# A Griffin-style encoder step on one core: splits in two steps, loads and in-place sums set apart, buffers given homes that outlast a stage

## The chip, the cores and the metric

The kernel runs on one core of a Trainium2 chip. The metric is the device time of one execution in microseconds (us). The engines that matter are TensorE (PE for its matmuls, PEld for its weight loads), VectorE (DVE), ScalarE (ACT), GpSimd (POOL) and SyncE (SP). Each works through its own list of instructions in order and waits for the others by semaphores. SP issues nearly all loads, POOL issues most of the stores to scratch memory in the later stages.

## The reference

One layer of a streaming encoder is applied to 2048 frames of a new stream and to 64 frames of a running one; the kernel treats the 2112 frames as one row of columns, with channels in the partitions.

```python
proj = rmsnorm(x, norm_mix) @ w_in                       # 1024 -> 5632
x_rnn, y_gate, q, k, v, g_rnn, g_attn = jnp.split(proj, cuts, axis=-1)
h = rg_lru(causal_dwconv(x_rnn, ...), ...)               # a linear recurrence over time
y_attn = band_attention(rope(q), rope(k), v, sinks)      # chunks of 64, window 128
mixed = sigmoid(g_rnn) * h * gelu(y_gate) + sigmoid(g_attn) * y_attn
x = x + mixed @ w_out                                    # 1024 -> 1024
up = causal_dwconv(rmsnorm(x, norm_ffn) @ w_up, ...)     # 1024 -> 5632, three taps
gate, val = jnp.split(up, 2, axis=-1)
y = rmsnorm(x + (silu(gate) * val) @ w_down, norm_final) # 2816 -> 1024
```

All of it is float32, and the results (y, the key and value caches, the states) are float32.

## The kernel before

**Products.** A float32 operand is taken apart into a high part (ACT copies it, rounded, into an fp32r tile: `split`, L198) and a low part (DVE subtracts the high part from the source: L199). Each product is three matmuls, high by high, high by low, low by high. The function `split` issues both instructions one after the other, so the low part on DVE waits for ACT at once.

**Four stages.** (A) The product with `w_in`, the attention and the recurrence run over three sets of columns (`SETS`); here a scheduler orders the instructions by dependencies. From there on the order is the order in which the code is written ("manual schedule"). (B) The product with `w_out` runs in three phases, one for each pair of column blocks (`PAIRS`: 304, 304 and 448 columns a block). In a phase, `wout(i, m)` makes one of 8 output rows in two halves j; the weights come as 256 KB of `w_out`, are split (`wsplit`, L381) and kept in scratch `woS`, from which the later phases load them (`wload`, L371). Beside it run generators, driven a few steps at a time by `drive`: `mixes(p)` (L347) loads the rows of the mixed result for the next pair and splits them, `xprep(p)` (L769) loads the new residual rows, norms them, makes Strassen-like sums and splits those. `residual` (L848) adds the residual input, stores `x1S` and collects the squares for the norm. (C) The product with `w_up` goes by a plan of units; a unit has seven steps u, one of the seven block products of a Winograd scheme each (`Lane.product`, matmuls at L1040 to L1042). The first 20 units make their weights afresh and have two lanes (pairs 0 and 1, 24 matmuls a step); four units with one lane follow (12 matmuls a step), then 11 units of pair 2 with two lanes. `prepare` makes the weights a few steps ahead (raw loads L885, sums L907, splits; or a load of kept ones from `wuS`, L903). `Lane.after(u)` (L1079) takes the partial sums p1, p7 and V out of PSUM (ACT, L1087), adds (DVE, L1091 to L1098), starts the convolution (ACT L1070, DVE L1076), then SiLU (L1109), the gate (L1114) and the sums of the hidden rows (L1123 to L1132), which POOL stores to `hS` (L1119). `at(d, f)` puts a piece d steps later. (D) The product with `w_down` runs over seven products i and the pairs p, eleven k each (matmuls L1470 to L1472); `dweight` makes weights, `parts` splits hidden rows, and `side` drives the residual adds (`resid`), the squares (L1435 to L1439), the last norm (L737 to L739) and the outputs (L1452, L1454).

**Waits inside the lists.** Where an ACT split waits for its load, all that stands behind it on ACT waits too; the same holds for a DVE low part that waits for ACT. In stage B `mixes` has 8 row buffers for pair 0 and 2 for the others, raw weights have 2 buffers. In stage C the first 20 units have one buffer for V, so the second lane's V is taken one step later than the first's:

```python
if u in (0, 1) or u == 2 + (one and self.second_lane):
    i = min(u, 2)
    t = up["s"].tile([P, n], F32, name=("p1", "p7", "V")[i], bufs=1 if i == 2 and one else 2)
```

**Memory.** `Region` is a piece of SBUF that stays open while `Pool`s take slots from it by name. Region FW (23,712 bytes a partition) is opened only when stage A's pools are closed.

Of the kernel before, what the change touches and what calls it, by code (L numbers as in the profile page):

```python
# [126 lines left out]
def kernel(ctx: ExitStack, tc: tile.TileContext, xT, w_in, w_out, w_up, w_dn, gw, pk,  # L127
# [22 lines left out]
    es0 = ExitStack()  # L150
    wpool = es0.enter_context(tc.tile_pool(name="wpool", bufs=2))
# [48 lines left out]

    turn = [0]

    def kept(m, si):
# [6 lines left out]
        raw = wpool.tile([P, KO * P], F32, name="wraw", bufs=2)  # L210
# [25 lines left out]
    def stats(t0, n):  # L236
        r = rp_.tile([P, BN], F32, name="nr", bufs=2)[:, :n]
        s = rp_.tile([P, BN], F32, name="ns", bufs=2)[:, :n]
        for k in range(KO):
            x = xp.tile([P, BN], F32, name="xk", bufs=4)[:, :n]  # L240
# [15 lines left out]
    def apply(t0, n):  # L256
        hi, lo = xslots(t0)
        r = rstd[t0]
        for k in range(KO):
            x = xp.tile([P, BN], F32, name="xk", bufs=4)[:, :n]  # L260
# [86 lines left out]
    def mixes(i, xk):  # L347

        for t0, n in PAIRS[i]:
            xblocks[t0] = mixp[i].tile([P, KO, 2, n], F32R, name=f"x{t0}")  # L350
# [11 lines left out]
        yield  # L362
        for j, (k, t0, n) in enumerate(todo):
            split(xblocks[t0][:, k, 0], xblocks[t0][:, k, 1], raw[j])
            load()
            yield

# [11 lines left out]

    def wsplit(j):  # L380
# [7 lines left out]
    for si, blocks in enumerate(SETS):  # L388
# [282 lines left out]
        for g in range(4):  # L671
# [18 lines left out]
            if g == 3 and si == 2:  # L690

                es0.close()
                FW = Region(tc, "FW", 23712, F32)
                RA = Region(tc, "RA", 58368, F32R)
                mixp, wh0, raws, xk = [Pool(RA), None, None], Pool(RA), Pool(FW), Pool(FW)
                sums = [Pool(FW, right=i == 0) for i in range(3)]
                for i in (2, 1, 0):
                    sums[i].reserve("rs", PAIRS[i][0][1], 2)
                wh0.reserve("wh", 8 * P, 4)
                raws.reserve("wraw", 4 * P, 2)  # L700
                xk.reserve("xk", BS, 8)
# [3 lines left out]
                wload(1)  # L705
            for _ in at:
                if g == 3 and si == 2:
                    next(mixed)
# [58 lines left out]
    def put(p, o, k, src):  # L767
        split(xops[p, o][:, k, 0], xops[p, o][:, k, 1], src)

    def xprep(p, names, rs, tp):  # L770
# [16 lines left out]
        yield  # L787
        for k in range(4):
# [3 lines left out]
            for o in ("11", "21", "22"):  # L792
                if o in names:
                    put(p, o, k, x[o])
            yield
            nc.vector.tensor_tensor(x["11"], x["12"], x["11"], op=ALU.subtract)
            if xt is not None:
                nc.vector.tensor_tensor(x["12"], x["22"], x["12"], op=ALU.subtract)
                nc.vector.tensor_tensor(xt, x["22"], x["11"], op=ALU.subtract)
                load(k + 1, "22")  # L800
                nc.vector.tensor_tensor(x["21"], x["21"], xt, op=ALU.subtract)
                yield
                put(p, "T2", k, xt)
                put(p, "T4", k, x["21"])
                load(k + 1, "21")
                yield
            else:
                load(k + 1, "22", "21")
            if "T1" in names:
                put(p, "T1", k, x["11"])  # L810
            load(k + 1, "11")
            if xt is not None:
                put(p, "T3", k, x["12"])
            load(k + 1, "12")
# [5 lines left out]
    io, tp = [Pool(FW) for _ in phases], Pool(FW)  # L820

    wnext, xres = [3], {}
# [9 lines left out]
    def wout(i, m):  # L832
        work = [(t0, n, xres.pop((t0, m)), acc()) for t0, n in phases[i]]
        for j in (16 * i + 2 * m, 16 * i + 2 * m + 1):
            w = weights.pop(j)
# [8 lines left out]
            while wnext[0] < 48 and wnext[0] <= j + (4 if wnext[0] > 15 else 3):  # L844
                wload(wnext[0])
                wnext[0] += 1
        return work

    def residual(i, m, work):
        for t0, n, xr, ps in work:  # L850
            nc.vector.scalar_tensor_tensor(xr, ps[:, :n], 0.5, xr, op0=ALU.mult, op1=ALU.add)
            nc.gpsimd.dma_start(x1S[m, :, t0:t0 + n], xr)
            if m == 0:
# [33 lines left out]

    def wops(g, fresh):

        r = {"11": wraw(g, "11")}  # L890

        def parts(src):
            t = wh.tile([P, 2, 4 * P], F32R, name="wh")
            split(t[:, 0], t[:, 1], src)
            return t

        def kept_s(i, src):
            if fresh:
                t = parts(src())
                nc.gpsimd.dma_start(wuS[g, i], t.bitcast(F32))  # L900
            else:
                t = wh.tile([P, 2, 4 * P], F32R, name="wh")
# [7 lines left out]
        if fresh:  # L910
            r["21"] = wraw(g, "21")
        yield None
        r["22"] = wraw(g, "22")
        yield parts(r["11"])
        yield kept_s(0, lambda: comb("11", "11", "21", ALU.subtract))
        r["12"] = wraw(g, "12")
# [6 lines left out]
    def wsums(g, pool, out):  # L923

        for h in range(2):
# [5 lines left out]

            def keep(i, src):
                t = out.tile([P, 2, 2 * P], F32R, name="wx", bufs=2)
                split(t[:, 0], t[:, 1], src)
                nc.gpsimd.dma_start(wuS[g, i][:, :, h * 2 * P:(h + 1) * 2 * P], t.bitcast(F32))
# [6 lines left out]
            yield  # L942
            nc.vector.tensor_tensor(a, c, a, op=ALU.subtract)
            keep(1, a)
            yield
            nc.vector.tensor_tensor(b, b, c, op=ALU.add)
            keep(2, b)
            yield
            nc.vector.tensor_tensor(d, d, a, op=ALU.subtract)
            keep(3, d)  # L950
            yield

    def xsums(p, pool, width):
# [700 lines left out]
```

## Time and profile before

| what | value |
|---|---|
| median of 3 runs | 3159.97 us (3152.78 to 3161.12) |
| the profiled execution | 3154.25 us, span 3152.5 us |
| PE busy / DVE busy / ACT busy | 2909.8 / 2073.0 / 1547.2 us |
| matmuls | 17640 |
| mean granted TensorE clock | 0.965 |

The span is the time from the first to the last instruction; the execution's own time is 1.75 us more. A busy PE is not PE at its peak: a matmul at a lower granted clock is busy for longer. In a row of busy times by stretch, the columns are the stretch, its length, the busy time and the count of instructions of PE, PEld, DVE, ACT and POOL, the granted clock, the busy share of the 16 DMA engines and the GB/s that they moved. In a row of waits stand who waited, for whom, the total, how often, and the longest.

### The profile page before, as it was taken

How to read it: one execution, taken by the hardware profiler on the slowest of the kernel's cores; microseconds unless marked ns; L12 is line 12 of the kernel's file. 1: busy time of each engine (PE TensorE's matmuls, PEld its weight loads, DVE VectorE, ACT ScalarE, POOL GpSimd, SP SyncE). 2: the span in 40 equal slices, each digit the busy share in tenths (PEclk: the TensorE clock that was granted, in tenths of full speed). 3: DMA queues.
4: the chain of work that ended last, by engine and by line, in shares of the span. 5: the costliest groups of instructions: out<-in, count | busy, mean ns of one | idle time of the engine just before them, and what ended most of it. 6: DMA issues, size and time to landing. Idle time of an engine off the chain costs nothing. (4 is left out here: it accounts for less than half of the span.)

```text
span 3152.5 us, 48907 instructions
## 1 busy us (share of the span) xinstructions
PE 2909.8 (92%) x17640; PEld 2788.1 (88%) x17640; DVE 2073.0 (66%) x4048; ACT 1547.2 (49%) x3426; POOL 449.8 (14%) x655
## 2 busy tenths in 40 slices
PE   8999999999999999977887999889899998999996
PEld 7988889999989999976787899889799997899995
DVE  5388781577781777753567888777666556567666
ACT  4577662666751776642224444445444444333432
POOL 3231211000000000012211333222101111000001
PEclk9999999999999999987898999999999999999998
DMA  7776547444336444356654556555876666876653
GB/s 245 262 233 194 178 148 251 150 132 133 125 116 216 144 139 142 117 178 234 216 190 166 194 196 212 179 188 179 276 253 213 220 215 181 258 217 207 182 167 110
DMA packets 324499, 595.37 MB, mean 189 GB/s; under 512 B 37168, under 2 KB 224544, under 8 KB 307360
## 3 DMA queue, kind: packets, MB, share of 16 engines
q1 hardware_dynamic: 285728, 461.45, 46.1%
q0 software_dynamic: 38528, 130.79, 11.2%
q8 instruction: 139, 2.28, 0.3%
q14 instruction: 104, 0.85, 0.1%
HBM read 400.99 MB, written 191.64 MB: 188 GB/s over the span
## 5 line engine op out<-in xcount | busy, mean ns | idle before, releaser
L223 PE MATMUL mm<-xh,whl 128*128 128x320 f32 (+2 forms) x2112 | 689.7, 327 | 11.0 <-ACT xh L198 5.4
L224 PE MATMUL mm<-xl,whl 128*128 128x320 f32 (+2 forms) x2112 | 688.8, 326 | 7.4 <-DVE xl L199 4.7
L225 PE MATMUL mm<-xh,whl 128*128 128x320 f32 (+2 forms) x2112 | 686.5, 325 | 1.4 <-POOL whl L199 1.4
L198 ACT ACTIVATE RE<-FW 128x512 fp32r<-128x512 f32 (+2 forms) x540 | 290.1, 558 | 491.0 <-DVE FW L907 97.0
L199 DVE TENSOR_TENSOR RE<-FW,RE 128x512 fp32r<-128x512 f32 (+2 forms) x540 | 315.7, 602 | 210.8 <-ACT RE L198 209.0
L223 PEld LDWEIGHTS mm<-xh,whl 128*128 128x128 f32 x2112 | 401.3, 190 | 18.7 <-ACT xh L198 8.4
L224 PEld LDWEIGHTS mm<-xl,whl 128*128 128x128 f32 x2112 | 401.2, 190 | 16.6 <-DVE xl L199 7.1
L225 PEld LDWEIGHTS mm<-xh,whl 128*128 128x128 f32 x2112 | 401.8, 190 | 2.3 <-POOL whl L199 1.6
L1040 PE MATMUL mf<-RA,RE 128*128 128x304 f32 (+1 forms) x608 | 202.7, 333 | 37.9 <-ACT FA L1087 33.9
L1470 PE MATMUL mf<-RE 128*128 128x304 f32 (+2 forms) x616 | 198.2, 322 | 9.2 <-ACT RE L198 9.2
L1042 PE MATMUL mf<-RA,RE 128*128 128x304 f32 (+1 forms) x608 | 200.2, 329 | 0.3 <-DVE RE L199 0.2
L1041 PE MATMUL mf<-RA,RE 128*128 128x304 f32 (+1 forms) x608 | 199.5, 328 | 0.0
L1471 PE MATMUL mf<-RE 128*128 128x304 f32 (+2 forms) x616 | 198.4, 322 | 0.1
L1472 PE MATMUL mf<-RE 128*128 128x304 f32 (+2 forms) x616 | 196.9, 320 | 0.0
L1040 PE MATMUL mf<-RE 128*128 128x304 f32 (+1 forms) x488 | 161.1, 330 | 15.5 <-ACT FA L1087 11.7
L1042 PE MATMUL mf<-RE 128*128 128x304 f32 (+1 forms) x488 | 160.1, 328 | 0.1
L1041 PE MATMUL mf<-RE 128*128 128x304 f32 (+1 forms) x488 | 159.7, 327 | 0.0
L1040 PEld LDWEIGHTS mf<-RA,RE 128*128 128x128 f32 x608 | 116.2, 191 | 48.1 <-ACT FA L1087 40.2
L1076 DVE SCALAR_TENSOR_TENSOR FW<-FA,pkt,FW 128x608 f32<-128x608 f32 x176 | 146.2, 850 | 18.3 <-ACT FW L1070 15.2
L199 POOL TENSOR_TENSOR gl<-gr,gh 128x256 fp32r<-128x256 f32 x24 | 22.3, 930 | 788.7 <-ACT gh L198 788.7
L1040 PE MATMUL mm<-RE 128*128 128x304 f32 (+1 forms) x392 | 128.1, 327 | 3.3 <-DMA RE<-wuS 3.1
L1042 PE MATMUL mm<-RE 128*128 128x304 f32 (+1 forms) x392 | 126.9, 324 | 2.6 <-DVE RE L199 2.6
(339 smaller groups left out, 7313.0 us busy)
## 6 DMA issues: line engine op xcount, KB each, us to landing
whl<-wiS SPq DMA_DIRECT2D x88, 1024.0 KB, 5.2
RE<-wuS SPq DMA_DIRECT2D x104, 512.0 KB, 4.4
wiS<-whl SPq DMA_DIRECT2D x44, 1024.0 KB, 4.8
wuS<-RE POOLq DMA_DIRECT2D x80, 512.0 KB, 3.2
FW<-in_w_up_dram SPq DMA_DIRECT2D x158, 256.0 KB, 4.8
hS<-FA POOLq DMA_DIRECT2D x154, 152.0 KB, 3.9
FW<-hS SPq DMA_DIRECT2D x154, 152.0 KB, 2.9
wraw<-in_w_in_dram SPq DMA_DIRECT2D x44, 512.0 KB, 5.8
```

The lines of the kernel that those rows point to most:

```text
L198: nc.scalar.activation(hi, src, AF.Copy)
L199: (lo_eng or nc.vector).tensor_tensor(lo, src, hi.bitcast(F32), op=ALU.subtract)
L223: nc.tensor.matmul(ps[:, :n], wh[:, c], xh[:, k, :n], start=first, stop=False)
L224: nc.tensor.matmul(ps[:, :n], wh[:, c], xl[:, k, :n], start=False, stop=False)
L225: nc.tensor.matmul(ps[:, :n], wl[:, c], xh[:, k, :n], start=False, stop=last)
L1040: nc.tensor.matmul(ps[:, :n], w[:, 0, c], x[:, k, 0], start=first, stop=False, **more)
L1041: nc.tensor.matmul(ps[:, :n], w[:, 0, c], x[:, k, 1], start=False, stop=False, **more)
L1042: nc.tensor.matmul(ps[:, :n], w[:, 1, c], x[:, k, 0], start=False, stop=last, **more)
L1076: nc.vector.scalar_tensor_tensor(uc, G[:, j:j + self.cols], col("fw", 44 * j + m), uc, op0=ALU.mult, op1=ALU.add)
L1470: nc.tensor.matmul(ps[m][:, cs], w[:, 0, c], t[:, 0], start=k == 0, stop=False)
L1471: nc.tensor.matmul(ps[m][:, cs], w[:, 0, c], t[:, 1], start=False, stop=False)
L1472: nc.tensor.matmul(ps[m][:, cs], w[:, 1, c], t[:, 0], start=False, stop=k == 10)
```

## The change

The matmuls and what they compute stay; what moves is the place of the instructions in the lists, and the buffers.

- **Splits in two steps.** `split2` issues the high part on ACT and hands back a function that issues the low part on DVE. The callers keep it (`wlow`, `plow`, `dlow`, `low`) and issue it one step later: weights of `w_out` and `w_up`, hidden rows and weights of `w_down`, the rows of `mixes`, `xprep`, `xread`, `wsums`.
- **Stage B.** The generators are driven inside `wout`, after each half j (`besides`), two steps at a time, no longer after the residual (5 or 4 steps). `mixes(1)` has 5 row buffers, `mixes(2)` has 3 and moves from phase 0 to phase 1. Raw weights have 3 buffers and are loaded four halves ahead. The residual of row m-1 stands ahead of the product of row m.
- **First mixed rows early.** FW is opened at the start and also serves stage A. The 16 row loads of pair 0 and two `w_out` loads are written at the second head group of the third set, and the scheduler puts them around the change from the second to the third set, one weight load at the kernel's start. Their splits still go to region RA, which is opened where it was, in the room of stage A's weights and operands.
- **Stage C.** V has two buffers, and both lanes take it at u = 2. The pieces of the convolution are put one step later, ACT's part into `later` (ahead of the products), DVE's part into `then` (behind the preparing of weights). Raw weights are asked for one step earlier, in-place sums stand 3 to 6 steps behind the stores of the same tile. `xprep` of pair 1 is spread over the first four steps, five pieces of one k each. Of the 28 rows that `xread` brings for pair 2, 16 are split beside the one-lane units and 12 beside pair 2's first unit, as before; 19 loads stand in the one-lane units, before 16.
- **Stage D.** The first product goes over the pairs in the order 2, 0, 1; its raw weights are loaded from five steps before the end of stage C, and its weights and first hidden rows are made by the end. `side` takes two steps a k from the fifth product on. The order that emptied `side` at 33 steps before the end (L1497) is gone.

```diff
+    def split2(hi, lo, src):
+        nc.scalar.activation(hi, src, AF.Copy)
+        return lambda: nc.vector.tensor_tensor(lo, src, hi.bitcast(F32), op=ALU.subtract)
...
     def wsplit(j):
         if j < 16:
             weights[j] = t = wh0.tile([P, 2, 4 * P], F32R, name="wh")
-            split(t[:, 0], t[:, 1], wraws.pop(j))
-            nc.gpsimd.dma_start(wpart(j), t.bitcast(F32))
+            low = split2(t[:, 0], t[:, 1], wraws.pop(j))
+            wlow.append(lambda: (low(), nc.gpsimd.dma_start(wpart(j), t.bitcast(F32))))
...
-    def wout(i, m):
+    def wout(i, m, beside):
         work = [(t0, n, xres.pop((t0, m)), acc()) for t0, n in phases[i]]
         for j in (16 * i + 2 * m, 16 * i + 2 * m + 1):
+            while wlow:
+                wlow.pop(0)()
...
-            while wnext[0] < 48 and wnext[0] <= j + (4 if wnext[0] > 15 else 3):
+            while wnext[0] < 48 and wnext[0] <= j + 4:
                 wload(wnext[0])
                 wnext[0] += 1
+            beside()
...
-            residual(i, m, work)
-            drive(side, 5 if i == 0 else 1 if m == 0 else 4)
+            work = wout(i, m, besides if i == 0 or m > 0 else lambda: drive(side, pace[0] if i == 1 else 0))
...
-            if u in (0, 1) or u == 2 + (one and self.second_lane):
-                i = min(u, 2)
-                t = up["s"].tile([P, n], F32, name=("p1", "p7", "V")[i], bufs=1 if i == 2 and one else 2)
+            if u in (0, 1, 2):
+                name = ("p1", "p7", "V")[u]
+                t = up["s"].tile([P, n], F32, name=name)
...
-                self.uv = self.conv_a(self.Gv, vm)
-                at(1, lambda: self.conv_b(self.Gv, vm, self.uv))
+                at(1, lambda: setattr(self, "uv", self.conv_a(self.Gv, vm)))
+                at2(1, lambda: self.conv_b(self.Gv, vm, self.uv))
...
     def prepare(i):
+        while plow:
+            plow.pop(0)()
...
+           for p in ((2, 0, 1) if i == 0 else (0, 1, 2) if i < 6 else (2, 1)) for k in range(11)]
...
         if j == len(seq) - 33:
-            drive(side, 99)
             nc.scalar.activation(warm, epst, AF.Sqrt)
```

**How the lists move.** ACT in phase 0 of stage B, before. RA with 128x512 is a half of the weights, RE and RC with 128x304 or 128x448 are mixed rows of pairs 1 and 2, L858 squares a residual row.

```order
L198 ACTIVATE RE<-FW 128x304 x5
L198 ACTIVATE RA<-FW 128x512 x2
L858 ACTIVATE FW<-FW 128x304 x2
L198 ACTIVATE RE<-FW 128x304 x2
L198 ACTIVATE RE<-FW 128x448
L198 ACTIVATE RC<-FW 128x448
L198 ACTIVATE RA<-FW 128x512 x2
```

ACT at the same place now; `split2` is L205, the squares are L880 and L883.

```order
L205 ACTIVATE RE<-FW 128x304
L205 ACTIVATE RA<-FW 128x512
L205 ACTIVATE RE<-FW 128x304 x2
L880 ACTIVATE FW<-FW 128x304 x2
L205 ACTIVATE RA<-FW 128x512
L205 ACTIVATE RE<-FW 128x304 x2
L205 ACTIVATE RA<-FW 128x512
```

Ahead of two halves of the weights stood five or four mixed rows; now two rows stand between one half and the next, and the 448-wide rows are gone from this phase.

ACT in one of the 20 fresh units, steps u = 0 to 4, before. L198 is the high part of the weights being prepared, L1087 takes p1, p7 or V out of PSUM, L1109 is SiLU.

```order
L198 ACTIVATE RE<-FW 128x512
L1087 ACTIVATE FA<-mf 128x304 x2
L1109 ACTIVATE FA<-FW 128x608 x2
L198 ACTIVATE RE<-FW 128x512
L1087 ACTIVATE FA<-mf 128x304 x2
L198 ACTIVATE RE<-FW 128x512
L1087 ACTIVATE FA<-mf 128x304
L198 ACTIVATE RE<-FW 128x512
L1087 ACTIVATE FA<-mf 128x304
L198 ACTIVATE RE<-FW 128x512
```

The same steps now; L205 is the high part, L1137 the copy out of PSUM, L1153 SiLU.

```order
L205 ACTIVATE RE<-FW 128x512
L1137 ACTIVATE FW<-mf 128x304 x2
L1153 ACTIVATE FA<-FA 128x608 x2
L205 ACTIVATE RE<-FW 128x512
L1137 ACTIVATE FW<-mf 128x304 x2
L205 ACTIVATE RE<-FW 128x512
L1137 ACTIVATE FW<-mf 128x304 x2
L205 ACTIVATE RE<-FW 128x512 x2
```

The second lane's V stood behind the next weights, one step after the first lane's; now the two stand together.

DVE near the end of stage D, before. L1439 adds squares, L1505 adds the last product of pair 1, L739 is the reciprocal of the norm, L1452 writes outputs.

```order
L1439 TENSOR_TENSOR FD<-FD 128x304 x3
L1505 TENSOR_TENSOR RR<-mf,RR 128x304 x4
L199 TENSOR_TENSOR RE<-FW,RE 128x304
L1439 TENSOR_TENSOR FD<-FD 128x304 x3
L1439 TENSOR_TENSOR FD<-FD 128x448 x7
L739 RECIPROCAL FD<-FD 128x448
L1452 SCALAR_TENSOR_TENSOR RR<-RR,pkt,FD 128x448 x8
L1439 TENSOR_TENSOR FD<-FD 128x304 x4
L739 RECIPROCAL FD<-FD 128x304
```

The same place now; L206 is the low part of hidden rows, L1558 adds squares, L1631 is the product's add, L754 the reciprocal, L1571 the outputs.

```order
L1558 TENSOR_TENSOR FD<-FD 128x448
L206 TENSOR_TENSOR RE<-FW,RE 128x304
L1558 TENSOR_TENSOR FD<-FD 128x448 x6
L1631 TENSOR_TENSOR RR<-mf,RR 128x304 x4
L206 TENSOR_TENSOR RE<-FW,RE 128x304 x3
L754 RECIPROCAL FD<-FD 128x448
L1571 SCALAR_TENSOR_TENSOR RR<-RR,pkt,FD 128x448
L206 TENSOR_TENSOR RE<-FW,RE 128x304
L1571 SCALAR_TENSOR_TENSOR RR<-RR,pkt,FD 128x448 x2
```

Before, the squares and the whole output of one block stood in one piece behind the last product of pair 1; now the squares stand ahead of that product's adds, and the low parts of hidden rows, which the next matmuls need, stand between the outputs.

More of the change, by code (lines that the diff above doesn't have):

```diff
@@ L1351 @@
             f()
+        if lanes[0] == (0, 2) and u == 3:
+            for pool in up["c"], up["u"], up["h"]:
+                pool.close()
+            up["c"], up["u"], up["h"] = Pool(FA), Pool(FA), Pool(FP)
+            up["c"].reserve("G", 2 * BM + 2, 3)
+            up["u"].reserve("uc", 2 * BM + 2, 4)
         for lane in live:
             lane.product(u, ready[i, lane.g])
-        while made <= i + ahead:
+        while made < len(plan) + 1 and fits(i):
             prepare(made)
             made += 1
+        for f in then.pop(i, ()):
+            f()
         for lane in live:
@@ L1405, in flushing @@
     def flushing():
[L1406 to L1410 removed]
+        for f in due():
+            f()
+            yield
     dp = R = None
```

484 lines of the change are left out of this document (285 added, 199 removed).

## The prediction

> **What bounds the kernel now.** I read the page's head first, then the span in slices, then the busy times cut at the stages' borders, then the waits inside each stretch.
>
> ```profile
> span 3152.5 us, 48907 instructions
> PE 2909.8 (92%) x17640; PEld 2788.1 (88%) x17640; DVE 2073.0 (66%) x4048; ACT 1547.2 (49%) x3426; POOL 449.8 (14%) x655
> PE   8999999999999999977887999889899998999996
> PEclk9999999999999999987898999999999999999998
> ```
>
> PE bounds the kernel, with 92% of the span. What an order can win lies where the PE slices fall below 9: slices 18 to 22 and 26 to 29 (stages B and C), 34 (the start of stage D), and the last. In most of the same slices the granted clock falls too. The stretches, cut at the stage borders, show by how much; the last two lie in the middle of undisturbed work and give the pace.
>
> ```profile
> 1369.80:1479.30 109.50, 74.99 (x384) 70.56 (x385) 41.98 (x84) 33.38 (x71) 28.82 (x48) 0.74 0.68 223
> 1479.30:1554.40 75.10, 60.92 (x391) 60.00 (x390) 44.30 (x95) 21.69 (x49) 17.47 (x32) 0.89 0.70 229
> 1554.40:1635.90 81.50, 79.06 (x390) 72.78 (x389) 42.56 (x81) 17.13 (x35) 17.53 (x32) 1.00 0.65 213
> 1635.90:1693.20 57.30, 34.20 (x198) 32.39 (x198) 38.66 (x65) 18.81 (x44) 5.40 (x10) 0.76 0.45 150
> 1693.20:2197.90 504.70, 463.05 (x3170) 453.65 (x3169) 394.41 (x680) 238.52 (x564) 150.20 (x276) 0.97 0.55 191
> 2197.90:2263.60 65.70, 53.68 (x338) 51.08 (x337) 43.56 (x73) 32.71 (x75) 10.18 (x19) 0.92 0.82 267
> 2263.60:2642.00 378.40, 375.41 (x1850) 346.74 (x1848) 232.65 (x340) 173.57 (x427) 39.81 (x74) 1.00 0.67 222
> 2642.00:2710.00 68.00, 51.23 (x313) 48.88 (x313) 38.96 (x69) 26.77 (x60) 7.37 (x14) 0.90 0.76 224
> 2710.00:3060.00 350.00, 349.36 (x2141) 335.86 (x2140) 227.87 (x444) 133.06 (x273) 11.51 (x22) 1.00 0.70 208
> 3060.00:3152.50 92.50, 61.91 (x403) 57.49 (x401) 53.57 (x103) 21.88 (x53) 13.44 (x25) 0.84 0.31 97
> 1700.10:1713.60 13.50, 13.47 (x96) 13.47 (x97) 10.82 (x20) 5.02 (x13) 4.81 (x9) 1.00 0.53 189
> 2320.00:2400.00 80.00, 80.00 (x396) 74.16 (x395) 50.12 (x74) 33.49 (x84) 9.16 (x17) 1.00 0.68 223
> ```
>
> At clock 1.00 a 304-wide matmul takes 13.50/96 = 0.1406 us, a 448-wide one 80/396 = 0.202. Length less count times pace is what a stretch loses. Phase 0 of `w_out`: 109.5 - 384 x 0.1406 = 55.5. Phase 1: 75.1 - 391 x 0.1406 = 20.1. Phase 2: 81.5 - 390 x 0.202 = 2.7. The start of `w_up`: 57.3 - 27.8 = 29.5. The other fresh units: 504.7 - 445.7 = 59.0; at 168 matmuls a unit these are 18.87 units of 26.75 us, over a floor of 23.6. The one-lane units: 65.7 - 47.5 = 18.2. Pair 2 of `w_up` and the middle of stage D lose almost nothing (PE busy 375 of 378, 349 of 350). At the start of stage D, PE stands idle for 16.8.
>
> Part of each loss is clock, not idle time. Busy PE over the floor is 21.0 in phase 0, 5.9 in phase 1, 6.4 at the start of `w_up`, 17.4 in the fresh units, 6.2 in the one-lane units, together 57 us. The clock is low just where PE waited, so a wait that goes takes its share of this along. The Trainium skill, "TensorE: Matmul & The Clock Gate", section "What's actually happening", says that for modelling the ramp costs under 1% of a typical kernel's span, which here would be an estimate of 31.5 us; the trace does not agree, with 57 us in five stretches, since the ramp comes again after each long wait. By the page the sum below would be some 25 us less gain, 3057.
>
> **Phase 0 of `w_out`.** The waits in this stretch, the DMA issues by kind, and two ACT rows of the timeline:
>
> ```profile
> PE mf L840 <- ACT RA L198: 29.6, 6, 7.5
> PE mm L840 <- ACT RA L198: 9.2, 2, 4.9
> ACT RA L198 <- DMA FW<-in_w_out_dram: 30.6, 7, 6.0
> ACT RE L198 <- DMA FW<-mixS: 24.0, 9, 4.1
> FW<-mixS SPq DMA_DIRECT2D x16, 224.0 KB, 2.6
> 1385.86 0.97 ACT L198 ACTIVATE RE<-FW 128x304 fp32r<-128x304 f32 x2 [4.07 <-DMA FW<-mixS]
> 1389.86 0.61 ACT L198 ACTIVATE RA<-FW 128x512 fp32r<-128x512 f32 x1
> ```
>
> PE waits 38.8 us for the high parts of weights, and ACT, which makes them, stands 24.0 us at mixed rows whose loads have not landed and 30.6 at raw weights. The timeline shows one case: a mixed row waits 4.07 us, and the weights behind it come at 1389.86. The change puts two rows ahead of a half where four or five stood, more row buffers behind them, a third raw-weight buffer, and the 16 rows of pair 2 elsewhere. What then ends last is the transfer of bytes: 109.5 us x 223 GB/s = 24.4 MB, less 16 x 224 KB = 3.7 MB, leaves 20.7 MB. The densest stretch, the one-lane units, moved 267 GB/s at a share of 0.82, so 326 at a full one. 20.7 MB take 77.6 us at 267 and 63.6 at 326; these are my bounds (gain 32 to 46). I take 73.5, in the lower half, since here the transfers have more buffers than in the one-lane units: **-36**.
>
> The first product of this phase I put at 0. Its rows come earlier, but their splits go to the same region as before, which opens only when the last product of `w_in` is done, and the same 16 high parts stand ahead of the first weights.
>
> **Phases 1 and 2.** Phase 1 takes in the 16 wide rows: 75.1 x 229 = 17.2 MB become 20.9, which need 64 us at 326 and 78 at 267, so the transfers take up what the waits give. DVE gets 16 low parts more on its 44.3 us, near 10 by the row of low parts below, and stays under 55. I take 0, with ends at -11 and +8. Phase 2: **-1**, of 2.7 at most.
>
> **The start of `w_up`.** These rows are waits of the stretch 1635 to 1694:
>
> ```profile
> PE mf L1040 <- ACT FA L1087: 23.1, 3, 9.1
> DVE FA L790 <- DMA FA<-x1S: 5.6, 2, 3.1
> ACT RE L198 <- DVE FW L907: 10.3, 4, 5.5
> ```
>
> PE idles 23.1 us in three waits for PSUM banks that ACT has not yet emptied. ACT is held by DVE, whose list here holds the norm and `xprep` of pair 1 in large pieces (38.7 of 57.3 busy; rows wait for loads, 5.6). The change spreads those pieces over four steps. DVE's 38.7 us of work must still be done in the stretch, and that is a floor for it unless pieces move out; 41 us leaves two us for loads. **-16**, with bounds 0 and -25 (the 23.1 and a share of the 6.4 of clock).
>
> **Fresh units.** Waits of the stretch 1693 to 2198, and two groups of DVE's instructions:
>
> ```profile
> PE mf L1040 <- ACT FA L1087: 21.3, 22, 2.6
> PE mm L1040 <- ACT FA L1087: 17.0, 9, 4.3
> ACT FA L1087 <- DVE FA L1091: 22.8, 19, 1.2
> ACT RE L198 <- DVE FW L907: 86.7, 39, 4.4
> DVE RE L199 <- ACT RE L198: 74.5, 104, 1.9
> L199 DVE TENSOR_TENSOR RE<-FW,RE 128x512 fp32r<-128x512 f32 (+2 forms) x540 | 315.7, 602 | 210.8 <-ACT RE L198 209.0
> L1076 DVE SCALAR_TENSOR_TENSOR FW<-FA,pkt,FW 128x608 f32<-128x608 f32 x176 | 146.2, 850 | 18.3 <-ACT FW L1070 15.2
> ```
>
> PE waits 38.3 us for copies out of PSUM. Nineteen of these copies wait for DVE's use of the one V buffer (22.8 us), near one a unit; behind them in ACT's list stand the next high parts. ACT itself waits 86.7 us for weight sums, and DVE 74.5 for high parts: the two engines take turns. With two V buffers both copies stand at u = 2 and wait only for PE; with low parts a step later DVE no longer waits for a high part issued just before. What is late next is DVE: 394.4/18.87 = 20.9 us of work a unit, under the 23.6 of PE, so PE can be the bound, with 2.7 us a unit of room. I take 24.55 a unit, one us above the floor for steps in which DVE has more than its mean: 2.2 x 18.87 = **-42**. Bounds: 0 (the turns stay) and -59.
>
> What is moved here is not free on DVE. The product's third matmuls need the low part, now made a step after the high part; it stands ahead of the next sums, and whoever waits for it is PE. The cover is that weights are prepared several steps ahead; if that went, it is the slower rival below.
>
> **One-lane units and stage D.** Waits of 2198 to 2264, of 2640 to 2710, then of 3060 to the end:
>
> ```profile
> PE mf L1040 <- DMA RE<-wuS: 4.8, 3, 3.1
> PE mf L1470 <- ACT RE L198: 9.2, 1, 9.2
> PE mf L737 <- DVE FD L1439: 10.7, 1, 10.7
> PE mm L737 <- DVE FD L1439: 8.9, 2, 7.0
> ```
>
> The one-lane units move 65.7 x 267 = 17.5 MB; the change takes none of it out (three row loads more), and at 326 it needs 54 us. PE waits for these loads. **-5**, between 0 and -12.
>
> The first product of stage D waits 9.2 us for a high part that stands behind its loads. Weights and rows made by the end of stage C take that away and part of the remaining idle time: **-12** of 16.8 idle us, bounds 0 and -19 with some clock. The work goes beside the end of pair 2, where ACT is busy 174 of 378 us and DVE 233; cost there: 0, at most the 3 us of idle PE that it has.
>
> In the last stretch PE waits 19.6 us for sums of squares that stood in one piece on DVE, ahead of the low parts. With the emptying order gone, the low parts stand between the outputs and `side` goes at two steps a k. DVE has 53.6 us of work in 92.5, and its outputs still end the kernel. **-13**, bounds 0 and -25.
>
> **Stage A.** Sixteen row loads and two weight loads now stand in SP's list at the change from the second to the third set. Those loads that wait for a store hold what is behind them on SP, and that is the weights and rows of the third set.
>
> ```profile
> FW<-mixS SPq DMA_DIRECT2D x32, 152.0 KB, 3.0
> ```
>
> One takes 3.0 us to land. If the loads behind have been asked for early enough it costs nothing; if five of the sixteen held PE for the 4.07 us seen above it would cost 20. **+3**, near the lower end because PE's slices there are all 9: the weights come well ahead.
>
> **Sum.** -36 + 0 - 1 - 16 - 42 - 5 - 12 - 13 + 3 = -122. From the profiled execution's own 3154.25 this gives **3032**. That execution is 0.2% under the median of 3159.97 and within the runs; I leave the sum on it. About 0.3%, 9.5 us, is what a measurement of this kernel can tell from no change.
>
> **Rivals.**
> *The fresh units stay in turns* (chance 0.20). The order of ACT and DVE changes, but each still waits for the other once a step: the 86.7 us for sums do not hang on the low part. Then -42 goes: 3074. Against it: the 22.8 us at one buffer are named and go.
> *Nearly every wait goes* (0.08). Phase 0 at 326 GB/s (-10 more), phase 1 at 64 (-11), fresh units at 23.8 (-14), the start of `w_up` (-8), the rest (-8): -51 more, about 2980. Against it: DVE at 88% of such a unit.
> *The late low parts hold PE* (slower, 0.09). A convolution's two adds on both lanes, 4 x 0.85 us, together with two low parts, 2 x 0.6, and the weight sums make 4.6 us and more of DVE work in one step; PE's step is 24 x 0.1406 = 3.4. Low parts come behind that. If three steps of a unit wait 2.7 us each, a unit takes 24.55 + 8 = 32.6 us and the time is 3032 + 151 = 3183. It decides from a unit of 31.5 us, which is 131/18.87 = 7.0 over my forecast. For it: DVE's share of 78% in these units. Against it: the mean step has 3.0 us of DVE work, and weights are ahead.
> *The waits only change places* (0.06). Bytes and DVE work are all still there, so the early rows and early weights are paid back where the loads collide, and it stays within 10 us of 3154. Against it: the transfers' share is 0.55 in the fresh units, which lose most.
>
> **How the numbers follow.** My forecast has the rest, 0.57, with its own range from 2990 to 3070 by the terms' bounds (half of the -42 or half of the -36 back, or some 40 more). The range from 2975 to 3100 takes in that, the first rival, and the second's upper part; it leaves out the last two and the edges. Faster: 0.57 + 0.20 + 0.08 + 0.02 = 0.87; same 0.04; slower 0.09.
>
> **What would show it.** In the changed profile: phase 0 near 73 us with a transfer share over 0.8, and PE's waits there for ACT's RA under 10 us in all; a fresh unit near 24.5 us with clock 1.00 and DVE busy near 21 of it; no wait of PE for a V copy; the start of `w_up` near 41; the waits for sums of squares under 7; stage A ending at 1370 to 1375. It would be wrong if a fresh unit stayed over 26 us, if PE waited there for low parts, or if phase 0 kept 100 us with ACT waiting for raw weights: then transfers, not the order of ACT, were its limit.

## The result, and the profile after

The changed kernel takes 3043.99 us (median of 4 runs, 3039.19 to 3044.68) against 3158.85 for the kernel before; the ratio is 0.9636, with a 95% interval of 0.9619 to 0.9653. The profiled execution took 3043.69 us, its span is 3041.9, so 110.6 us of span are gone. The head of the page and its slices after the change:

```profile
span 3041.9 us, 48860 instructions
PE 2886.8 (95%) x17640; PEld 2764.9 (91%) x17640; DVE 2064.7 (68%) x4048; ACT 1541.4 (51%) x3426; POOL 450.5 (15%) x655
PE   8999999999999999998797999999899999999998
PEclk9999999999999999998898999999999999999999
```

The matmuls are the same 17640 and PE is busy for 23 us less: part of what was busy before ran at a granted clock of 0.50 (142 us of busy PE before, 91 us now, by the clock's own records in the two traces). DVE and ACT have the same work. Of the low slices 18 to 22 three are left (19, 20 and 22, stage B and the start of `w_up`); 26 and 27 in the fresh units and 34 at the start of stage D are gone, 29 holds the one-lane units, and the last is at 8 where it was at 6. The same stretches as before, ending at the same matmuls; the last four rows run from the end of `w_up`'s last matmul (2558.0) through the first product of `w_down`, the five whole products, the rest to the end, and 80 us of undisturbed pair 2:

```profile
1371.80:1442.60 70.80, 60.02 (x385) 58.41 (x386) 31.66 (x67) 20.75 (x45) 28.99 (x48) 0.89 0.85 293
1442.60:1521.80 79.20, 60.92 (x390) 59.72 (x389) 50.93 (x107) 27.64 (x62) 15.39 (x29) 0.87 0.74 245
1521.80:1602.00 80.20, 80.20 (x390) 72.87 (x389) 45.98 (x86) 18.79 (x38) 20.16 (x37) 1.00 0.69 229
1602.00:1654.30 52.30, 34.56 (x197) 31.99 (x196) 36.82 (x63) 18.76 (x45) 4.84 (x9) 0.77 0.47 156
1654.30:2110.30 456.00, 447.19 (x3171) 442.39 (x3170) 388.99 (x675) 234.64 (x558) 149.18 (x274) 1.00 0.60 210
2110.30:2175.40 65.10, 50.59 (x338) 48.57 (x338) 43.44 (x74) 33.65 (x77) 10.69 (x20) 0.97 0.86 289
2175.40:2558.00 382.60, 381.89 (x1849) 346.58 (x1848) 231.65 (x343) 171.02 (x423) 40.82 (x76) 1.00 0.64 217
2558.00:2632.10 74.10, 69.21 (x399) 64.85 (x398) 44.74 (x77) 32.80 (x72) 8.08 (x15) 0.93 0.84 253
2632.10:2953.50 321.40, 318.40 (x1986) 306.76 (x1985) 212.81 (x418) 124.83 (x257) 10.18 (x19) 1.00 0.70 211
2953.50:3041.90 88.40, 73.64 (x473) 68.80 (x472) 61.19 (x119) 25.50 (x60) 13.42 (x25) 0.96 0.36 116
2320.00:2400.00 80.00, 80.00 (x389) 72.67 (x388) 48.46 (x71) 36.04 (x87) 9.67 (x18) 1.00 0.63 211
```

For stage D the stretches of the prediction end at other matmuls, so these are the three parts of the kernel before at the same matmuls:

```profile
2641.80:2727.10 85.30, 68.53 (x398) 64.73 (x397) 49.54 (x86) 31.74 (x69) 9.17 (x17) 0.92 0.80 238
2727.10:3045.70 318.60, 317.96 (x1986) 306.74 (x1986) 209.35 (x414) 124.74 (x257) 9.72 (x18) 1.00 0.69 207
3045.70:3152.50 106.80, 76.22 (x473) 70.75 (x471) 61.70 (x118) 25.23 (x59) 13.44 (x25) 0.87 0.32 100
```

| part | before | after | difference | forecast |
|---|---|---|---|---|
| stage A | 1369.8 | 1371.8 | +2.0 | +3 |
| `w_out`, phases 0, 1, 2 | 109.5, 75.1, 81.5 | 70.8, 79.2, 80.2 | -38.7, +4.1, -1.3 | -36, 0, -1 |
| start of `w_up` | 57.3 | 52.3 | -5.0 | -16 |
| other fresh units | 504.7 | 456.0 | -48.7 | -42 |
| one-lane units | 65.7 | 65.1 | -0.6 | -5 |
| pair 2 of `w_up` | 378.2 | 382.6 | +4.4 | 0 |
| first product of `w_down`, with the wait ahead | 85.3 | 74.1 | -11.2 | -12 |
| five whole products | 318.6 | 321.4 | +2.8 | 0 |
| the rest | 106.8 | 88.4 | -18.4 | -13 |
| sum | | | -110.6 | -122 |

The longer pair 2 is not the work of the change: its matmuls run at the slower of two paces here, of which the last section tells, and most runs below have the other one.

What PE still waits for in the fresh units (1654 to 2110), and at the start of `w_up` (1600 to 1656), there with DVE's own first wait:

```profile
PE mf L1092 <- ACT FW L1137: 7.6, 10, 1.4
PE mm L1092 <- ACT FW L1137: 0.2, 1, 0.2
```

```profile
PE mf L1092 <- ACT RE L205: 9.6, 2, 6.9
PE mf L1094 <- DVE RE L206: 4.1, 1, 4.1
DVE FA L811 <- DMA FA<-x1S: 9.1, 4, 3.7
```

The 38.3 us of waits for copies out of PSUM are 7.8, and the clock there is 1.00. At the start of `w_up` the copies gave way to the weights' high and low parts, 13.7 us, and DVE waits longer than before for residual rows.

### The profile page after: what moved, and what is told of

It is laid out like the page before. It is cut to its first block, busy times and chain, and to the rows that moved or that the text cites. A ratio compares the mean times of both kernels' runs of the same rounds, so it can differ in the third digit from the quotient of the medians.

```text
span 3041.9 us, 48860 instructions
## 1 busy us (share of the span) xinstructions
PE 2886.8 (95%) x17640; PEld 2764.9 (91%) x17640; DVE 2064.7 (68%) x4048; ACT 1541.4 (51%) x3426; POOL 450.5 (15%) x655
## 5 line engine op out<-in xcount | busy, mean ns | idle before, releaser
L205 ACT ACTIVATE RE<-FW 128x512 fp32r<-128x512 f32 (+3 forms) x556 | 296.8, 554 | 475.1 <-DVE FW L934 114.9
L206 DVE TENSOR_TENSOR RE<-FW,RE 128x512 fp32r<-128x512 f32 (+3 forms) x556 | 319.9, 596 | 104.4 <-ACT RE L205 103.5
L1128 DVE SCALAR_TENSOR_TENSOR FA<-FA,pkt 128x608 f32<-128x608 f32 (+1 forms) x264 | 245.9, 951 | 71.6 <-ACT FA L1122 67.0
L1092 PE MATMUL mf<-RA,RE 128*128 128x304 f32 (+1 forms) x608 | 201.4, 331 | 10.6 <-ACT FW L1137 8.2
L1122 ACT ACTIVATE FA<-FA,pkt 128x608 f32<-128x608 f32 (+1 forms) x132 | 128.4, 973 | 110.4 <-DVE FA L1143 104.2
L1092 PE MATMUL mm<-RE 128*128 128x304 f32 (+1 forms) x392 | 125.4, 320 | 7.2 <-ACT FW L1137 4.4
```

The costliest lines, as they stand in the source:

```text
L205: nc.scalar.activation(hi, src, AF.Copy)
L206: return lambda: nc.vector.tensor_tensor(lo, src, hi.bitcast(F32), op=ALU.subtract)
L1092: nc.tensor.matmul(ps[:, :n], w[:, 0, c], x[:, k, 0], start=first, stop=False, **more)
L1128: nc.vector.scalar_tensor_tensor(uc, G[:, j:j + self.cols], col("fw", 44 * j + m), uc, op0=ALU.mult, op1=ALU.add)
```

## The experiments

Each kernel was timed in three rounds beside the kernel before, which ran at 3160 to 3162 us; what counts is its ratio to that, against 0.9636 (0.9619 to 0.9653) for the whole change.

### The fresh units: which part of the change

**One V buffer again** (on the changed kernel).

```diff
-            if u in (0, 1, 2):
-                name = ("p1", "p7", "V")[u]
+            if u in (0, 1) or u == 2 + (n < BM and self.second_lane):
+                name = ("p1", "p7", "V")[min(u, 2)]
...
-            up["s"].reserve(name, n, 2)
+            up["s"].reserve(name, n, 1 if name == "V" and n < BM else 2)
```

> The changed kernel, with one V buffer in the fresh units again and the second lane's V taken a step after the first's. My theory (the one buffer held ACT, and with it PE): a good part of the 49 us that the fresh units gained goes, 20 to 40 us, so 3064 to 3084 in all, and PE waits there for the V copy again. Rival (the turns between ACT and DVE were what counted, and they are undone by the other edits): under 8 us, 3044 to 3052.

3042.7 us, ratio 0.9631 (0.9616 to 0.9645): no difference. The fresh units take 457.7 us. My theory of the buffer falls in the changed kernel: PE waits 9.1 us for copies in the fresh units with one buffer and 7.8 with two. A second buffer alone, on the kernel before, was not tried.

**Low parts of the weights of `w_up` at once** (on the changed kernel).

```diff
-            plow.append(split2(t[:, 0], t[:, 1], src))
+            split(t[:, 0], t[:, 1], src)
...
-                low = split2(t[:, 0], t[:, 1], src())
-                plow.append(lambda: (low(), nc.gpsimd.dma_start(wuS[g, i], t.bitcast(F32))))
+                split(t[:, 0], t[:, 1], src())
+                nc.gpsimd.dma_start(wuS[g, i], t.bitcast(F32))
```

> The changed kernel, with the low part of each weight of w_up issued at once behind its high part. My theory (two steps spare DVE its waits for ACT): DVE waits again near 70 us for high parts, and the fresh units lose 10 to 25 us: 3054 to 3069. Rival (weights are several steps ahead, so DVE's wait costs PE nothing): within 5 us of 3044.

3104.0 us, ratio 0.9833 (0.9811 to 0.9854): 60 us slower than with the whole change, more than I expected and more than the fresh units had gained. The stretch, and the waits of PE, DVE and ACT in it:

```profile
1654.50:2170.50 516.00, 463.19 (x3170) 455.50 (x3170) 390.00 (x679) 233.92 (x560) 149.58 (x274) 0.97 0.54 186
```

```profile
PE mf L1092 <- ACT FW L1137: 38.4, 20, 3.4
PE mm L1092 <- ACT FW L1137: 13.0, 8, 3.2
DVE RE L201 <- ACT RE L200: 110.5, 94, 3.1
ACT RE L200 <- DVE FW L934: 125.1, 40, 6.9
ACT FA L1153 <- DVE FA L1128: 43.6, 32, 1.8
```

The 60 us are all here (516.0 against 456.0). PE waits for copies out of PSUM as before the change, though there are two V buffers: DVE stands 94 times for a high part just issued, and its other work comes later for that. ACT, in whose list the copies stand, then waits for DVE in two places: for the weights' sums (125.1 us, 107.2 in the changed kernel) and, in the last row, with SiLU (L1153) for the convolution's adds (L1128): 43.6 us, where it is 8.8 in the changed kernel and 8.5 in the kernel before. The name in PE's row is that of the last link. The wait of SiLU grew the most, and it is small in the kernel before, where low parts are issued at once too but the convolution is early. So the 60 us are the price of low parts at once beside a late convolution; that would fit a stretch longer than the 504.7 us before the change, but no run splits the two.

**The convolution at once** (on the changed kernel).

```diff
-                at(1, lambda: setattr(self, "uv", self.conv_a(self.Gv, vm)))
-                at2(1, lambda: self.conv_b(self.Gv, vm, self.uv))
+                self.uv = self.conv_a(self.Gv, vm)
+                at(1, lambda: self.conv_b(self.Gv, vm, self.uv))
```

(the same for the gate's half)

> The changed kernel, with ACT's part of the convolution issued right behind the sums, and DVE's part ahead of the products, as before the change. My theory (V buffers and low parts make the gain): 0 to 10 us slower, 3044 to 3054. Rival (ACT standing at the convolution for DVE's sums held the copies out of PSUM, and that is where the gain of the fresh units came from): 15 to 40 us slower, 3059 to 3084.

3049.5 us, ratio 0.965 (0.9632 to 0.9669). The interval overlaps that of the change, so the total alone doesn't tell; the stretch does, 470.1 us against 456.0, and its waits of PE:

```profile
PE mf L1094 <- DVE RE L206: 10.3, 13, 1.2
PE mm L1094 <- DVE RE L206: 4.8, 5, 1.2
```

The convolution's adds stand ahead of the low parts here, and PE waits 15.1 us for these. That is the slower rival's mechanism (late low parts hold PE) at a small price; in the changed kernel the adds stand behind the low parts and there is no such wait. So the size is near my expectation, while neither account had named this wait. In this execution later stretches gave back most of the 14 us, 7 of them pair 2 at its other pace.

**Low parts a step later, alone** (on the kernel before).

```diff
             t = wh.tile([P, 2, 4 * P], F32R, name="wh")
-            split(t[:, 0], t[:, 1], src)
+            nc.scalar.activation(t[:, 0], src, AF.Copy)
+            plow.append(lambda: nc.vector.tensor_tensor(t[:, 1], src, t[:, 0].bitcast(F32), op=ALU.subtract))
...
     def prepare(i):
+        while plow:
+            plow.pop(0)()
```

(the store of a kept weight goes with its low part)

> The kernel before, with one part of the change alone: the low part of each weight of w_up is issued at the next preparing, a step after its high part. Theory from the run that undid this part (the turns between ACT and DVE held the copies out of PSUM): 35 to 60 us less than before, 3100 to 3125. Rival (it works only together with the earlier raw loads, the later convolution and the second V buffer): under 15 us less, 3145 or more.

3158.5 us, ratio 0.9983 (0.9964 to 1.0002): no gain, as the rival said. The stretch, PE's waits, and one of DVE's (L897 is the low part here, L1091 the copy, L1074 ACT's part of the convolution):

```profile
1698.00:2201.30 503.30, 464.28 (x3171) 452.06 (x3170) 393.56 (x680) 238.06 (x564) 150.55 (x277) 0.98 0.54 192
```

```profile
PE mf L1046 <- DVE RE L897: 13.5, 11, 1.8
PE mm L1044 <- ACT FA L1091: 8.3, 9, 1.7
PE mm L1046 <- DVE RE L897: 8.0, 7, 1.4
PE mf L1044 <- ACT FA L1091: 7.1, 16, 1.8
DVE FW L1080 <- ACT FW L1074: 29.9, 19, 2.0
```

The copies' 38.3 us fall to 15.4, as the theory wanted; 21.5 us of waits for low parts take their place, and DVE now stands 29.9 us (10.9 before) for the convolution. So the late low part is needed for the gain and is not enough: something else must bring it early enough. The later convolution is one such part, by the run above. If it acts here as it does there, it explains about 14 of the 47 us between this kernel's 503.3 and 456.0; whether the earlier raw loads and the spaced sums make the rest, and whether the two parts together would do on the kernel before, was not tried.

### Phase 0 of `w_out`

**Pair 2's mixed rows in phase 0 again, two row buffers a pair** (on the changed kernel).

```diff
-            xk.reserve("xk", BS, 5)
-            side, pace = [mixes(1, xk)], (2, 0)
+            xk.reserve("xk", BS, 2)
+            xk2 = Pool(FW)
+            xk2.reserve("xk", BM, 2)
+            side, pace = [mixes(1, xk), mixes(2, xk2)], (3, 0)
...
-            side, beside, pace = [mixes(2, xk)], [xprep(0, ORDER, rsum, tp)], (2, 2)
+            side, beside, pace = [], [xprep(0, ORDER, rsum, tp)], (2, 2)
```

> The changed kernel, with the mixed rows of pair 2 brought and split in phase 0 again, and two row buffers for each of the pairs there. Theory that bytes bound phase 0 (24.4 MB instead of 20.7, at 282 to 326 GB/s): phase 0 5 to 13 us longer, phase 1 down by 4 or more, about 3044 to 3052 in all. Rival (ACT standing at mixed rows bounds it): ACT waits for rows near 24 us again, phase 0 25 us longer or more, 3060 and over.

3064.6 us, ratio 0.9691 (0.9662 to 0.972). Phases 0 and 1, and waits of phase 0:

```profile
1370.60:1486.30 115.70, 73.88 (x384) 70.94 (x385) 40.85 (x83) 30.12 (x61) 28.93 (x48) 0.78 0.67 218
1486.30:1548.30 62.00, 56.63 (x391) 56.05 (x390) 41.81 (x91) 20.35 (x47) 15.22 (x28) 0.94 0.73 241
```

```profile
ACT RE L205 <- DMA FW<-mixS: 61.8, 22, 6.5
DVE RE L206 <- ACT RE L205: 53.3, 19, 6.6
PE mf L865 <- DVE RA L206: 33.4, 9, 7.8
```

Phase 0 is 45 us longer and phase 1 17 us shorter, 28 us together; the total shows 21, since pair 2 is 7 us shorter at its other pace. The byte theory falls for this kernel: 115.7 us x 218 GB/s = 25.2 MB would take 86 us at the 293 GB/s that phase 0 reached after the change. ACT stands 61.8 us at rows that have not landed, and the chain goes on through DVE's low parts to PE. Phase 0 is even longer than the 109.5 us before the change, though the splits in two steps, the third buffer for raw weights and the early rows are all still there; alone they gain nothing in this phase. The edit undoes three things at once: the place of the rows, the buffers, and the steps a half, which go from two to three; which counts for more is open.

### The start of `w_up`

Here the forecast was far off, so three runs on the changed kernel look for what is late.

**The norm of pair 2 three steps later.**

```diff
-            if i == 1:
-                norms(2)
...
+        if i == 4:
+            norms(2)
```

(with its stores, and the sums closed behind it)

> The changed kernel, with the norm of pair 2 (two reciprocals on DVE) moved from the second step of w_up to the fifth, behind the last pieces of pair 1. My theory of what is left of the 52 us at the start of w_up (the reciprocals stand ahead of low parts and pieces that PE needs next): 5 to 10 us less, 3034 to 3039. Rival (the row loads that DVE waits for set the pace there): within 3 us of 3044.

**Two buffers for each residual row of pair 1's last pass.**

```diff
+            if two:
+                x = dict(nx)
+                load(k + 1, *where)
             for o, (half, t) in where.items():
                 nc.vector.scalar_tensor_tensor(x[o], x[o], ...)
```

(`load` takes a new tile `nx[o]` with `bufs=2`)

> The changed kernel, with two buffers for each of the four residual rows in the last pass over pair 1, so that the next rows are loaded while the last are worked on. Theory that the loads set the pace at the start of w_up: 6 to 12 us less, 3032 to 3038. Rival (DVE's reciprocals and pieces set it): within 3 us of 3044.

**Both.**

> Both of the edits at the start of w_up: norm of pair 2 later, and two buffers for the rows. If each has its own wait: the sum of the two, 11 to 20 us less, 3024 to 3033. If one cause stands behind both: no more than the better of the two.

The norm alone: 3040.6 us, ratio 0.9619 (0.9599 to 0.9639), no difference that can be told. The rows alone: 3034.3, ratio 0.9597 (0.9572 to 0.9623). Both: 3027.9, ratio 0.9574 (0.955 to 0.9598), clear of the change's interval. The stretch in each, in this order:

```profile
1602.00:1654.40 52.40, 34.40 (x198) 31.06 (x198) 34.42 (x59) 15.04 (x35) 4.32 (x8) 0.80 0.41 135
```

```profile
1601.80:1645.60 43.80, 33.46 (x198) 31.17 (x197) 36.38 (x63) 18.54 (x45) 4.84 (x9) 0.84 0.55 184
```

```profile
1602.80:1644.50 41.70, 33.21 (x199) 29.79 (x198) 34.18 (x59) 15.20 (x35) 4.32 (x8) 0.88 0.52 170
```

And DVE's wait for the rows, with the norm later, then with both:

```profile
DVE FA L811 <- DMA FA<-x1S: 12.6, 4, 6.2
```

```profile
DVE FA L818 <- DMA FA<-x1S: 1.9, 1, 1.9
```

With the norm gone from DVE's list, DVE reaches the rows sooner and waits 12.6 us for them, 9.1 with the norm in place: the loads set the pace. Two buffers take 8.5 us off the stretch, and then two more go with the norm. With both edits this is the fastest version tried, 16 us under the changed kernel; 10.6 of these are in the stretch, and in the profiled execution pair 2 is 6.5 us shorter at its other pace, which is not the edits' work.

### The end, and stage D

**The emptying order put back** (on the changed kernel), and **taken out alone** (on the kernel before).

```diff
         if j == len(seq) - 33:
+            drive(side, 99)
```

```diff
         if j == len(seq) - 33:
-            drive(side, 99)
```

> The changed kernel, with the order that empties the side work 33 steps before the end put back. My theory (the sums of squares in one piece ahead of the low parts held PE at the end): 10 to 18 us slower, 3054 to 3062. Rival (with two steps a k the side work is nearly empty by then, so there is nothing left to pile up): within 4 us of 3044.

> The kernel before, with one part alone: without the order that empties the side work 33 steps before the end. Theory (that order made the 19.6 us of waits for sums of squares): 8 to 15 us less than before, 3145 to 3152. Rival (one step a k leaves the side work to be done at the very end, where nothing hides it): no gain or slower, 3158 and over.

Put back: 3048.5 us, ratio 0.9654 (0.9633 to 0.9675), not to be told from the change by the total. Taken out alone: 3148.8, ratio 0.9956 (0.9939 to 0.9974), 11 us under the kernel before beside it, as the theory said. The stretch that starts with the last product, with the order put back and with it taken out, and PE's first wait with it put back:

```profile
2945.60:3043.90 98.30, 74.50 (x474) 70.14 (x472) 61.58 (x119) 25.56 (x60) 13.49 (x25) 0.89 0.33 104
3050.60:3144.70 94.10, 73.18 (x474) 69.19 (x472) 60.87 (x118) 24.93 (x59) 13.44 (x25) 0.90 0.37 114
```

```profile
PE mf L752 <- DVE FD L1558: 10.8, 1, 10.8
```

Put back, it takes 9.9 us more than the 88.4 of the changed kernel; taken out, 12.7 less than the 106.8 of the kernel before. So in the profiles the two directions roughly agree. The median with the order put back shows only 4.5 us, in intervals that hold either; in its profiled execution pair 2 is 8 us shorter at its other pace, which hides most of the loss. The rest of the 18.4 is not split further.

**The first product over the pairs 0, 1, 2** (on the changed kernel).

```diff
-           for p in ((2, 0, 1) if i == 0 else (0, 1, 2) if i < 6 else (2, 1)) for k in range(11)]
+           for p in ((0, 1, 2) if i < 6 else (2, 1)) for k in range(11)]
```

> The changed kernel, with the first product of stage D over the pairs in the order 0, 1, 2 again. My theory (the weights and rows made by the end of stage C brought the 11 us; the wide pair first gives the next loads more time): 3 to 8 us slower, 3047 to 3052. Rival (the order has no part in it): within 3 us of 3044.

3043.5 us, ratio 0.9626 (0.9605 to 0.9647): no difference in the total. The stretch of the first product, over the same number of matmuls, says otherwise:

```profile
2554.80:2634.60 79.80, 67.62 (x397) 64.23 (x397) 49.34 (x85) 33.18 (x75) 8.78 (x17) 0.94 0.87 259
```

It takes 79.8 us against 74.1, and the nine other runs on the changed kernel have 69.6 to 74.3 there. PE waits 12.1 us in it for high and low parts, 5.3 in the changed kernel. So about half of the 11.2 us hangs on the order, near what my theory said. The total hides it, since pair 2 takes 375.7 us in this execution, at its other pace, against 382.6. That the other half comes from the weights made ahead remains argued, not shown.

### The one-lane units

**Rows of pair 2 split one a step** (on the changed kernel).

```diff
-                for _ in range(2):
+                for _ in range(2 if u % 4 == 0 else 1):
                     if raw2[0] < 17:
```

> The changed kernel, with the rows of pair 2 beside the one-lane units split one a step (two at every fourth) and no longer two a step until they are done. Theory (ACT stands at a row whose load has not landed, and the copies out of PSUM stand behind it): 3 to 8 us less in the one-lane units, 3036 to 3041. Rival (the bytes of these units bound them, whatever the order): within 3 us of 3044.

3040.8 us, ratio 0.9616 (0.9583 to 0.9648); the stretch takes 64.1 us against 65.1, and ACT still waits for the rows:

```profile
ACT RA L205 <- DMA FP<-xS: 12.6, 5, 3.2
```

Nothing to be told in the total, and the wait did not go. The bytes (65.1 us x 289 GB/s = 18.8 MB, at a transfer share of 0.86) fit the rival; it is not proved by this.

## Why the prediction was right, and where it was not

**The likeliest case came, 12 us beside the forecast** (3044 for 3032), within its own range of 2990 to 3070. That it came so near is in part luck, since errors of both signs lie in it: the start of `w_up` gave 11 us less than forecast, and 4 to 5 us each were missing in phase 1, the one-lane units and pair 2 (there by its pace); the fresh units gave 7, the end 5 and phase 0 3 more than forecast. In all some 27 us too hopeful and 16 too careful.

**Clock.** The forecast that a wait takes its share of clock along held. PE busy over the floor, by the rows above and the same pace of 0.1406 us: 5.9 in phase 0, 6.1 in phase 1, 6.9 at the start of `w_up`, 1.4 in the fresh units, 3.1 in the one-lane units, 23 us together where it was 57. That is 34 us of the 110.6 by this measure. The clock's own records in the traces, which hold 1.00 and 0.50 and nothing between, give a little less: PE was busy at 0.50 in these five stretches for 97 us before and 38 after, and half of that, 48 and 19 us, is lost, so 29 us of the gain are clock there. In the whole kernel the loss went from 71 to 46 us, 25 less, since stage A loses 6 us more than before. The Trainium skill, "TensorE: Matmul & The Clock Gate", section "What's actually happening", has the ramp penalty at under 1% of a typical kernel's span. All the loss in the traces is more than that, 2.3% before (71 of 3152.5 us) and 1.5% after (46 of 3041.9). But the page speaks there of the first matmuls of a kernel, and here most of the loss comes after later waits: the first 100 us have 4.7 of the 71 and 5.5 of the 46. So my prediction set two different things side by side, and these traces don't contradict the page.

**Phase 0: right size, and half of the reason.** I let the bytes bound it at 282 GB/s; it moved 293 at a share of 0.85. But the run with the rows put back shows that the bytes were not what the older order lost to: the 45 us came with ACT standing at rows, at a lower rate of bytes (218 GB/s). Phase 1 came out 4.1 us longer than the forecast's 0, within its ends; PE waits there for kept weights, the transfers that took up the gain.

```profile
PE mf L863 <- DMA RE<-woS: 11.5, 3, 7.7
PE mm L863 <- DMA RE<-woS: 6.8, 1, 6.8
```

**Start of `w_up`: the step that failed** is "41 us leaves two us for loads". One buffer for each residual row leaves DVE standing for loads four times, 9.1 us. The run with both edits came to 41.7 us, but DVE has 34.2 us of work there and not 38.7, so it does not show that DVE's work was the floor. My bounds of 0 and -25 held the 5.0.

**Fresh units: right sum, wrong part.** "Nineteen of these copies wait for DVE's use of the one V buffer" was true of the trace, and the buffer still is worth nothing in the changed kernel (457.7 against 456.0). What the runs show to be needed is the low part a step later, by which DVE waits 10.5 us for high parts where it waited 74.5 (first row); alone it is not enough:

```profile
DVE RE L206 <- ACT RE L205: 10.5, 15, 1.1
```

```profile
ACT RE L205 <- DVE FW L934: 107.2, 50, 6.2
```

I had named this as the second cause, and not that it needs other parts beside it. ACT still waits for sums, more than before (the second row, 107.2 for 86.7), without harm, so the first rival read the wrong row too. With 24.2 us a unit PE is the bound, as forecast.

**Stage D: the sum was right.** The start gave 11.2 for 12, but I gave it all to weights and rows made ahead, and about half hangs on the order of the pairs. At the end the waits for sums of squares fell from 19.6 us to 3.2, as forecast (under 7); the term was 5 us too small.

```profile
PE mm L752 <- DVE FD L1558: 2.1, 2, 1.2
PE mf L752 <- DVE FD L1558: 1.1, 1, 1.1
```

**Rivals.** The turns, "nearly every wait goes" and "only change places" did not come. The late low parts are real, since both runs with the convolution ahead of them show PE waiting for them, 15 and 21.5 us; the changed kernel escapes by its order.

## What to carry to other kernels

- A row "PE waits for ACT's copy" names the last link. Follow the list of the engine named, what it stands at, and what that engine stands at: with low parts at once the cause was two links back, in subtracts that waited for a copy just issued.
- Undo one part of a working change and do one part alone: a part can be needed and still bring nothing by itself, as the late low parts did (60 us undone, nothing alone).
- Where two versions are close, compare the stretch that the edit touches before the total: the order of the pairs in stage D cost 5.7 us in its stretch and nothing in the total, because another stretch ran at another pace.
- Where a wait goes and the stage stays as long, look for the next in the same list: the norm moved away only showed the loads behind it; with both mended the stage fell by a fifth.

## What the runs showed of the hardware

The wide matmuls of pair 2 have two paces at clock 1.00, without a wait. 80 us in the middle of pair 2 hold 389 of them in three of the fourteen profiled executions (the changed kernel, the low parts alone, two buffers for the rows) and 396 or 397 in the eleven others. The rows are those of the low parts alone and of the first product's order, both from 2320 to 2400:

```profile
2320.00:2400.00 80.00, 80.00 (x389) 72.66 (x388) 45.06 (x68) 33.88 (x86) 8.07 (x15) 1.00 0.64 209
```

```profile
2320.00:2400.00 80.00, 80.00 (x397) 74.16 (x396) 49.68 (x72) 37.67 (x92) 9.68 (x18) 1.00 0.65 219
```

That is 0.2057 or 0.2015 us a matmul, 2%, some 8 us over pair 2. It goes with no edit that I can name. It is more than the 4.4 us that pair 2 lost here: nine of the runs on the changed kernel have the faster pace, and eight of these take 374.4 to 376.2 us for pair 2, less than the 378.2 before (the ninth, 380.7, moves splits into it). So it blurs every difference of a few us between single executions; what pace the executions without a trace had is not known. What sets it stays open.
